# Two-layer hybrid trunk, first layer: the second half's token projections in one go, attention released behind its q part, small opening loads issued by ScalarE

## The chip, the cores and the metric

The kernel runs on one core of a Trainium2 chip. The metric is the device time of one execution in microseconds, the median of three runs. PE is TensorE, ACT is ScalarE, DVE is VectorE, POOL is GpSimd and SP is SyncE, which issues nearly all DMA transfers here.

## What is computed

Two layers over 1024 tokens of width 1024, all in float32. Each layer, shortened from the reference:

```python
xn = rmsnorm(h, attn_norm_g)
za, zq, zk, zv, zc = split(xn @ w_in)          # 512, 512, 128, 128, 256 columns
ya = chunk_gmlp(za, ...)                       # 4 heads, chunks of 128 tokens
yb = swa_sink_attention(rope(q), rope(k), v)   # 8 query heads, 2 kv heads, window 128
yc = s5_ssm(zc, ...)                           # 16 groups, then a gated output
h = h + concat[rmsnorm(ya), rmsnorm(yb), rmsnorm(yc)] @ w_out
h = h + square(relu(rmsnorm(h) @ w_ff1)) @ w_ff2          # 4096 wide
h = h + sigmoid(rmsnorm(h) @ w_ple_gate) * (p[i] @ w_ple_proj)
```

## The kernel before

The tokens are cut into two halves of 512 (h = 0 and 1), and activations stand with channels on the partitions: `X[h]` holds the input of the next product as a high and a low part (`split_scaled`, ACT for the high part at L89, DVE for the low one at L90). A product is three passes of 128x512 matmuls (`cm`, L359). Weights come through a ring: SP loads a piece of 512 KB into `st`, ACT writes its high part (L104) and DVE its low part (L105); `main_plan` fixes the order of the pieces.

The kernel is written as generators ("lanes"). `main` runs one generator and lets every other lane take steps in proportion (`tick`); flags hold a lane back (`wait`). What this emits is then put in order, engine by engine, by a scheduler, and each engine works its own list strictly in that order. SP's list matters as much as the others: a transfer that has to wait holds all transfers behind it.

The stretch that the change touches comes first. `first_x` loads x (tiles `xt`) and makes `X[0]` and `X[1]`. `project0` then does the input projection of both halves: token parts (`z_tok`, L710) give rows of tokens and have two parts, part 0 (the gMLP's v columns, k and v; weights in two pieces of 64-column strips) and part 1 (q). Channel parts (`z_chan`) give rows of channels, m = 0 and 1 for the S5 input `zu`, m = 2 and 3 for the gMLP's u, `za`. The order is: half 0 part 0, half 0 part 1, half 1 part 1 with kept weights, channel parts 0 and 1, half 1 part 0, channel parts 2 and 3. All results go to DRAM through tiles of the tag `z`, with two buffers in the pool `zs`; from the flag "zg" on, two more stand in the pool `pz`.

Beside that the lanes run: the S5 tables and `ssm(0, 0)` (it waits for the flag ("zu", 0, 0) and uses PSUM bank "x"), `gmlp(0, 0)` (bank "x" as well), and `attention(0, 0)`, which is started after "zg" and works in eight units of a block and a kv head: `pq` (L1188), `pss` (L1201), softmax, `pt` (L1238), `po` (L1259). Its outputs are written into `X[0]`, so before the first `attn_sum` it waits until the projection no longer reads `X[0]` (flag ("z", 0, 0)).

After `project0` comes `embed`: it loads p in eight tiles `ptk` (tag `z` too), transposes them (L811), and makes the products with `w_ple_proj` for both layers in 32 pieces of six matmuls, each copied by ACT to a tile `pjz` (tag `z`, L825) and stored by SP (L826). `mix_out(0, 0)` follows, the product of the three normed parts in `X[0]` with `w_out`; its first three output blocks are begun on the gMLP and attention rows alone. From there on the kernel is a row of windows, large products with the other lanes' work between them.

## Time and profile before

| what | value |
|---|---|
| median of 3 runs | 2381.09 us (2380.5 to 8480.06) |
| profiled execution, own time | 2385.95 us |
| profiled execution, span in the trace | 2384.2 us |
| PE busy over the span | 2325.3 us |
| PE idle between 0 and 300 us (from its busy time in stretches of 20 us) | 31.8 us |

A trace shows each engine's instructions with start and duration in us from the span's start, and in brackets how long the engine had been idle and what ended that. The clock PEclk is the granted TensorE clock as a share of 2.4 GHz; its lower level, 1.2 GHz, is 0.5.

### The profile page before, as it was taken

What the parts mean: (1) busy time and instruction counts of PE and PEld (TensorE: products, weight loads), DVE (VectorE), ACT (ScalarE), POOL (GpSimd) and SP (SyncE); (2) the same over time, 40 slices, a digit from 0 to 9 for tenths busy, and PEclk for the clock granted to TensorE, in tenths of its full rate; (3) what the DMA queues carried; (4) which work ended last, traced back from release to release, by engine and by line L of the source; (5) the groups of instructions that cost most, each with busy time, mean ns of one, the idle gap of its engine ahead of it and who ended that gap; (6) DMA issues with size and microseconds to landing.
All of it is one profiled execution on the core that took longest, in us unless ns stands there. A gap on an engine that the chain in (4) does not pass through costs nothing.

```text
span 2384.2 us, 29265 instructions
## 1 busy us (share of the span) xinstructions
PE 2325.3 (98%) x10941; PEld 1885.4 (79%) x10941; DVE 1552.8 (65%) x2700; ACT 1027.8 (43%) x1787; POOL 5.4 (0%) x15
## 2 busy tenths in 40 slices
PE   7998899999999999999999999999999999999998
PEld 5886687788788887777888888777888887888887
DVE  7877767675966765676585774676657674444455
ACT  7427646433334443553342543464334343322333
POOL 0000000000000000000000000000000000000000
PEclk9998999999999999999999999999999999999999
DMA  8663632253553335324443344522534334333333
GB/s 244 188 203 119 208 99 64 80 173 106 145 156 102 111 125 155 95 78 140 123 135 124 98 145 124 145 72 76 166 105 135 124 97 134 97 96 94 94 97 98
DMA packets 403558, 295.94 MB, mean 124 GB/s; under 512 B 66668, under 2 KB 376024, under 8 KB 401624
## 3 DMA queue, kind: packets, MB, share of 16 engines
q1 hardware_dynamic: 403416, 294.07, 41.1%
q8 instruction: 86, 1.41, 0.3%
q14 instruction: 56, 0.46, 0.1%
HBM read 250.48 MB, written 43.54 MB: 123 GB/s over the span
## 4 chain that ended last, share of the span: by engine, by line
PE 83%; DMA 7%; DVE 5%; ACT 3%; issue 2%; SPq 1%; ACTq 0%; DVEq 0%
PE mm_ps L359 43%; PE x_ps L359 20%; PE s_ps L359 8%; DMA st<-in_w_in 2%; DVE w L105 2%; PE s_ps L710 1%; PE po L1259 1%; PE pss L1201 1%; ACT w L104 1%; PE p_ps L359 1%; DMA st<-in_w_out 1%; PE p_ps L947 1%; DMA yu<-ye 1%; PE pt L1238 1%; SPq L98 1%
## 5 line engine op out<-in xcount | busy, mean ns | idle before, releaser
L104 ACT CAST w<-st 128x1024 fp32r<-128x1024 f32 x364 | 387.9, 1067 | 853.1 <-PE mm_ps L359 430.0
L359 PE MATMUL mm_ps<-x,w 128*128 128x512 f32 x2904 | 708.4, 396 | 7.9 <-ACT x L89 4.2
L359 PEld LDWEIGHTS mm_ps<-x,w 128*128 128x128 f32 x2904 | 544.5, 190 | 133.0 <-issue 10.1
L105 DVE TENSOR_TENSOR w<-st,w 128x1024 fp32r<-128x1024 f32 x364 | 448.5, 1234 | 202.6 <-ACT w L104 191.6
L359 PE MATMUL mm_ps<-A,w 128*128 128x512 f32 x2016 | 500.8, 392 | 2.5 <-DVE H L1333 2.5
L359 PEld LDWEIGHTS mm_ps<-A,w 128*128 128x128 f32 x2016 | 375.7, 188 | 85.4 <-DVE H L1333 4.9
L359 PE MATMUL x_ps<-A,w 128*128 128x512 f32 x1056 | 272.8, 393 | 4.1 <-DVE H L1333 4.1
L359 PE MATMUL x_ps<-x,w 128*128 128x512 f32 x1104 | 272.2, 394 | 0.0
L359 PE MATMUL s_ps<-x,w 128*128 128x512 f32 x1056 | 252.4, 391 | 4.8 <-DVE w L105 2.6
L359 PEld LDWEIGHTS x_ps<-x,w 128*128 128x128 f32 x1104 | 205.6, 188 | 45.6 <-issue 3.4
L359 PEld LDWEIGHTS s_ps<-x,w 128*128 128x128 f32 x1056 | 198.1, 188 | 49.1 <-DVE w L105 4.0
L359 PEld LDWEIGHTS x_ps<-A,w 128*128 128x128 f32 x1056 | 196.5, 188 | 51.0 <-DVE H L1333 8.3
L1333 DVE TENSOR_TENSOR H<-H,mm_ps 128x512 f32<-128x512 f32 x168 | 113.2, 683 | 84.2 <-PE mm_ps L359 83.3
L1344 DVE SCALAR_TENSOR_TENSOR r<-mm_ps,rbc 128x512 f32<-128x512 f32 x88 | 60.7, 690 | 119.2 <-PE mm_ps L359 119.2
L710 PE MATMUL s_ps<-w,x 128*128 128x512 f32 x384 | 101.3, 404 | 4.1 <-ACT x L89 2.6
L1333 DVE TENSOR_TENSOR H<-H,x_ps 128x512 f32<-128x512 f32 x88 | 60.2, 684 | 68.8 <-PE x_ps L359 68.2
L1348 DVE TENSOR_TENSOR A<-q,A 128x512 fp32r<-128x512 f32 x128 | 87.8, 686 | 6.8 <-ACT q L1347 6.6
L710 PEld LDWEIGHTS s_ps<-w,x 128*128 128x128 f32 x384 | 73.6, 194 | 20.8 <-ACT x L89 3.0
L1346 ACT ACTIVATE A<-r 128x512 fp32r<-128x512 f32 x128 | 80.2, 627 | 8.1 <-DVE r L1344 7.9
L1347 ACT ACTIVATE q<-r 128x512 f32<-128x512 f32 x128 | 78.9, 617 | 0.0
L1224 ACT ACTIVATE pr<-pr,anm,hf 128x128 f32<-128x128 f32 x128 | 61.6, 485 | 17.4 <-DVE anm L1221 17.4
L89 ACT ACTIVATE x<-H,gT 128x512 fp32r<-128x512 f32 x80 | 53.7, 711 | 13.5 <-PE s_ps L359 7.7
(386 smaller groups left out, 2112.3 us busy)
## 6 DMA issues: line engine op xcount, KB each, us to landing
st<-in_w_ff SPq DMA_DIRECT2D x256, 512.0 KB, 4.1
st<-in_w_out SPq DMA_DIRECT2D x32, 512.0 KB, 4.1
st<-in_w_ple_gate SPq DMA_DIRECT2D x32, 512.0 KB, 4.1
st<-in_w_in SPq DMA_DIRECT2D x18, 512.0 KB, 4.4
p<-par SPq DMA_DIRECT2D x8, 1024.0 KB, 8.5
pj<-pjz SPq DMA_DIRECT2D x32, 256.0 KB, 2.2
H<-hs SPq DMA_DIRECT2D x4, 2048.0 KB, 7.9
pj<-pj SPq DMA_DIRECT2D x32, 256.0 KB, 3.4
```

The lines of the kernel that those rows point to most:

```text
L89: self.S.activation(hi, x, AF.Copy, scale=g)
L98: self.Q.dma_start(sv[:, :, c0:c1], src)
L104: self.S.copy(hi, src)
L105: self.V.tensor_tensor(lo, src, hi.bitcast(F32), ALU.subtract)
L359: self.T.matmul(ps, w[:, i, k, c0:c0 + P], X[:, j, k, :], start=(start and n == 0), stop=(stop and n == last))
L710: T.matmul(pss[b], X[:, j, 2 * s + kk, c], w[:, i, kk, :], start=(s == 0 and kk == 0 and n == 0), stop=(s == 3 and kk == 1 and n == 2))
L1224: S.activation(pr[:, i], pr[:, i], AF.Exp, bias=nm[:, i:i + 1], scale=f[:, i:i + 1], accum_out=den[:, i:i + 1])
L1333: V.tensor_tensor(H[:, m], H[:, m], ps, ALU.add)
L1344: V.scalar_tensor_tensor(r, ps, 0.0, self.R[h][1], ALU.max, ALU.mult)
L1346: S.activation(A[:, 0, m], r, AF.Square)
L1347: S.activation(q, r, AF.Square)
L1348: V.tensor_tensor(A[:, 1, m], q, A.bitcast(F32)[:, 0, m], ALU.subtract)
```

## The change

Four things are edited. In `load_w` and `z_tok_plan` the four loads of 64-column strips become two, one for each 128 rows. `load_gains`, `rotary` and `ssm_tables` issue their eleven small loads from ACT. `project0` does the two token parts of half 1 one after the other, sets a new flag "zq1" after the q part, and does the four channel parts last; `run` starts the gMLP and attention lanes at "zq1", and the pool `pz` is gone. In attention the wait before the first `attn_sum` is gone; instead `attn_out` is put off until the flag is there, with two buffers for the held outputs `o` in this one place, and both pairs' factors `r` kept in one tile.

```diff
@@ load_w
         for c0, c1, src in pieces:
-            self.Q.dma_start(sv[:, :, c0:c1], src)
+            dst = sv[:, :, c0:c1]
+            if len(src.shape) == 4:
+                for k in range(a):
+                    self.Q.dma_start(dst[:, k].rearrange("p (j c) -> p j c", j=src.shape[2]), src[:, k])
+            else:
+                self.Q.dma_start(dst, src)
@@ z_tok_plan
-                pc = [(j * 64, j * 64 + 64, r[:, :, j * P + 64:(j + 1) * P]) for j in range(4)]
-                yield dict(pieces=pc + [(256, 512, r[:, :, 1024:1280])], a=2, b=512)
+                g = r[:, :, 0:512].rearrange("p k (j c) -> p k j c", j=4)[:, :, :, 64:P]
+                yield dict(pieces=[(0, 256, g), (256, 512, r[:, :, 1024:1280])], a=2, b=512)
@@ main_plan
-        chan = self.z_chan_plan(0)
-        yield next(chan)
-        yield next(chan)
         yield from self.z_tok_plan(0, 0)
-        yield from chan
+        yield from self.z_chan_plan(0)
@@ load_gains (rotary and ssm_tables alike)
-            Q.dma_start(rows[i * 16:(i + 1) * 16, :], a[nm].rearrange("l (k p) -> (l k) p", p=P))
+            S.dma_start(rows[i * 16:(i + 1) * 16, :], a[nm].rearrange("l (k p) -> (l k) p", p=P))
@@ project0
-        def chan(ms):
-            for m in ms:
-                w = F.next()
-                for h in range(2):
-                    yield from self.z_chan(0, h, m, w, "mm")
-
-        yield from chan((0, 1))
-        self.flags.add(("zu", 0, 0))
-        yield from self.z_tok(0, 1, 0, lambda s: F.next(), ss, ("p", "o", "s", "s"))
+        self.flags.add("zq1")
+        yield
+        yield from self.z_tok(0, 1, 0, lambda s: F.next(), ss, ("p", "mm", "o", "mm"))
         self.z_roots(0, 1, ss)
-        self.flags.add("zg")
-        yield
-        yield from chan((2, 3))
+        for m in range(4):
+            w = F.next()
+            for h in range(2):
+                yield from self.z_chan(0, h, m, w, "mm")
+            if m == 1:
+                self.flags.add(("zu", 0, 0))
@@ attn_steps
-                    yield from self.wait(("z", c["l"], h))
                     self.attn_sum(c, blk)
                     if blk % 2:
-                        late.append((p, blk - 1, self.attn_rstd(c)))
+                        late.append((p, blk - 1, c["o"], self.attn_rstd(c, blk % 4 // 2)))
...
-            if late and late[0][0] < p:
+            if late and late[0][0] < p and ("z", c["l"], h) in self.flags:
                 self.attn_out(c, *late.pop(0)[1:])
...
+        yield from self.wait(("z", c["l"], h))
+        for x in late:
+            self.attn_out(c, *x[1:])
+            yield
@@ attn_sum
-            c["o"] = at.tile([P, 2, 4, P], F32, name="o")
+            c["o"] = at.tile([P, 2, 4, P], F32, name="o", bufs=1 if c["l"] or c["h"] else 2)
@@ attn_rstd
-        r = c["at"].tile([P, 256], F32, tag="k", name="or")
+        if pair == 0:
+            c["r"] = c["at"].tile([P, 2, 256], F32, tag="k", name="or")
+        r = c["r"][:, pair]
@@ run
-        self.until(lambda: {"zg", "rotary"} <= self.flags)
+        self.until(lambda: {"zq1", "rotary"} <= self.flags)
         zws.close()
         self.lanes.remove(z0)
-        pzs = ExitStack()
-        self.zpools.append(self.pool(pzs, "pz", 2, side=self.side(0), reuse_waits="tile"))
...
-        self.zpools.pop()
-        pzs.close()
```

Three places of the two orders follow; lines of the changed kernel stand one to three away from those of before (L359 is L361 there, L1120 is L1118).

SP's list from its second load on, before: `pi` is the positions, `srows` and `ldr` the S5 inputs, `xt` a quarter of x.

```order
L98 DMA st<-in_w_in 128x2x64 x4
L98 DMA st<-in_w_in 128x2x256
L432 DMA rows<-in_attn_norm_g 16x128
L432 DMA rows<-in_mlp_norm_g 16x128
L432 DMA rows<-in_ple_norm_g 16x128
L432 DMA rows<-in_mix_out_g 16x128
L433 DMA rows<-in_ssm_d 4x128
L437 DMA sinks<-in_sinks 128x16
L443 DMA pi<-in_positions 8x128
L445 DMA inv<-in_inv_freq 128x32
L516 DMA srows<-in_ssm_a_re 16x128
L516 DMA srows<-in_ssm_a_im 16x128
```

And the changed kernel's, from the same place.

```order
L101 DMA st<-in_w_in 128x4x64 x2
L103 DMA st<-in_w_in 128x2x256
L477 DMA xt_196<-in_x 128x4x256
L101 DMA st<-in_w_in 128x4x64 x2
L103 DMA st<-in_w_in 128x2x256
L477 DMA xt_205<-in_x 128x4x256
```

The eleven small loads have left SP's list, and the second quarter of x moves up by thirteen issues. On ACT's list they stand before the first write of `X[0]`, five of them behind the first weight cast.

SP's list where the projection ends and `embed` begins, before (`yu` and `yt` are a store and a reload within `ssm`, `u<-za` the gMLP's load, `graw` the weights of the S5 output gate).

```order
L933 DMA graw<-in_glu_w 128x1x256 x4
L746 DMA za_138<-z 128x512
L806 DMA ptk<-in_p 128x2x256
L981 DMA u<-za_138 128x1024
L806 DMA ptk<-in_p 128x2x256
L908 DMA yu_131<-ye 128x512
L806 DMA ptk<-in_p 128x2x256
L910 DMA yt<-yu_131 128x8x64
L746 DMA za_139<-z 128x512
L806 DMA ptk<-in_p 128x2x256 x2
```

And the changed kernel's there.

```order
L748 DMA za_138<-z 128x512
L979 DMA u<-za_138 128x1024
L843 DMA u<-zu_123 128x512
L847 DMA p_2284<-par_118 128x2048
L906 DMA yu_130<-ye 128x512
L804 DMA ptk<-in_p 128x2x256
L908 DMA yt<-yu_130 128x8x64
L748 DMA za_139<-z 128x512
L804 DMA ptk<-in_p 128x2x256 x2
L103 DMA st<-in_w_out 128x8x128
L804 DMA ptk<-in_p 128x2x256 x5
```

The S5 lane now stands one half-group earlier in its own work at this place (`yu_130` is its first store, which before had gone long ago), and one `ptk` load stands ahead of the reload of `yu_130`, with seven behind it.

PE's list from the last products of `embed` to `mix_out`, before (`x_2240` is the operand of `embed`; `x_ps<-va` is the gMLP's sum of squares).

```order
L288 MATMUL x_ps<-va,onesr 128x512
L1201 MATMUL pss<-kT,qt 128x256 x8
L359 MATMUL mm_ps<-x_2240,w 128x512 x24
L1238 MATMUL pt<-identr,pr 128x128 x4
L359 MATMUL mm_ps<-x_2240,w 128x512 x12
L1259 MATMUL po<-pp,v 64x256 x2
L1259 MATMUL po<-pc,vd 64x256 x2
L1238 MATMUL pt<-identr,pr 128x128 x4
L359 MATMUL mm_ps<-x_2240,w 128x512 x12
L1259 MATMUL po<-pp,v 64x256 x2
L1259 MATMUL po<-pc,vd 64x256 x2
L359 MATMUL mm_ps<-x_2240,w 128x512 x12
```

And the changed kernel's (`x_2526` is the operand of `embed`, `x_2470` is `X[0]`).

```order
L1031 MATMUL psv<-wT,vg 64x128 x8
L361 MATMUL mm_ps<-x_2526,w 128x512 x12
L1031 MATMUL psv<-wT,vg 64x128 x8
L361 MATMUL mm_ps<-x_2526,w 128x512 x30
L290 MATMUL x_ps<-va,onesr 128x512
L361 MATMUL mm_ps<-x_2526,w 128x512 x6
L1118 MATMUL pk<-identr,kst 128x128 x20
L361 MATMUL mm_ps<-x_2470,w 128x512 x4
```

The gMLP's sum of squares now stands six matmuls ahead of the end of `embed`, where before 60 matmuls of `embed` followed it, and between `embed` and `mix_out` stand the 20 products `pk` of the next attention's keys.

## Rows read from the trace of the kernel before

**Rows 1.** Stretches: length, busy PE, PEld, DVE, ACT, POOL, PEclk, DMA share, GB/s.

```profile
0.00:50.00 50.00, 35.46 (x153) 26.83 (x153) 33.43 (x168) 40.25 (x106) 1.55 (x11) 1.00 0.78 231
102.00:183.00 81.00, 79.97 (x457) 67.16 (x456) 54.96 (x124) 25.17 (x43) 0.95 (x1) 1.00 0.72 205
183.00:211.00 28.00, 19.72 (x89) 17.20 (x88) 21.33 (x43) 20.19 (x50) 0.00 (x0) 0.70 0.45 138
211.00:289.00 78.00, 74.33 (x398) 55.03 (x397) 59.37 (x124) 60.95 (x145) 0.00 (x0) 1.00 0.45 152
289.00:294.50 5.50, 1.74 (x8) 1.12 (x6) 3.76 (x8) 1.38 (x4) 0.00 (x0) 0.84 0.85 344
339.00:365.00 26.00, 22.81 (x107) 19.04 (x106) 18.35 (x28) 15.46 (x29) 0.00 (x0) 0.92 0.26 82
```

**Rows 2.** SP's list in order of time, the opening.

```profile
1.29 2.54 SPq L98 DMA_DIRECT2D st<-in_w_in  x5
3.88 0.47 SPq L432 DMA_DIRECT2D rows<-in_attn_norm_g  x1
...
8.76 0.42 SPq L475 DMA_DIRECT2D xt<-in_x  x1
```

**Rows 3.** ACT's instructions in order of time.

```profile
9.42 1.27 ACT L89 ACTIVATE x<-mm_ps,gT 128x512 fp32r<-128x512 f32 x2 [1.43 <-DVE gT L436]
...
33.10 1.36 ACT L89 ACTIVATE x<-mm_ps,gT 128x512 fp32r<-128x512 f32 x2 [0.16 <-PE mm_ps L487]
...
185.25 0.63 ACT L212 ACTIVATE gelu_t<-u 128x512 f32<-128x512 f32 x1 [7.60 <-DMA u<-za]
```

**Rows 4.** PE's groups by line between 102 and 183 us: busy us, mean ns.

```profile
L359 PE MATMUL mm_ps<-x,w 128*128 128x512 f32 x192 | 46.1, 393 | 0.0
...
L904 PE MATMUL psY<-xp,p 128*128 128x128 f32 x32 | 5.4, 285 | 0.0
L906 PE MATMUL psY<-u,p 128*128 128x64 f32 x32 | 4.5, 262 | 0.0
```

**Rows 5.** PE's instructions in order of time.

```profile
222.70 1.19 PE L1201 MATMUL pss<-kT,qt 128*128 128x256 f32 x8
223.73 0.56 PE L1188 MATMUL pq<-identr,qst 128*128 128x128 f32 x4
...
227.04 0.65 PE L1259 MATMUL po<-pp,v 128*64 128x256 f32 x4
...
229.03 1.02 PE L288 MATMUL x_ps<-ssq,onesr 128*128 128x512 f32 x2
...
245.10 0.60 PE L1005 MATMUL pwt<-identr,wl 128*128 128x128 f32 x4
...
264.21 1.02 PE L288 MATMUL x_ps<-va,onesr 128*128 128x512 f32 x2
...
286.29 3.08 PE L359 MATMUL mm_ps<-x,w 128*128 128x512 f32 x12
289.21 1.52 PE L359 MATMUL s_ps<-x,w 128*128 128x512 f32 x6
294.52 2.07 PE L359 MATMUL mm_ps<-x,w 128*128 128x512 f32 x4 [3.78 <-ACT x L89]
```

**Rows 6.** SP's list in order of time, the first store and reload of `ssm`.

```profile
157.44 0.41 SPq L908 DMA_DIRECT2D yu<-ye  x1
...
166.06 0.37 SPq L910 DMA_DIRECT2D yt<-yu  x1
```

**Rows 7.** Instructions of the tile `pjz`: duration ns min/median/max, first and last start.

```profile
L825 ACT COPY pjz<-mm_ps x32: 563/587/650, 212.7 to 286.3; 128x512 f32<-128x512 f32 x32
...
DMA to landing us min/median/max: 2.0/2.2/6.2
```

**Rows 8.** DMA issues between 100 and 300 us: KB each, median us to landing.

```profile
ptk<-in_p SPq DMA_DIRECT2D x8, 256.0 KB, 3.4
```

**Rows 9.** DVE's instructions in order of time.

```profile
279.27 0.75 DVE L90 SCALAR_TENSOR_TENSOR x<-u,gT,x 128x512 fp32r<-128x512 f32 x1 [0.19 <-ACT x L89]
```

More of the change, by code (lines that the diff above doesn't have):

```diff
@@ L427, in load_gains @@
     def load_gains(self, t):
-        a, V, T, Q = self.a, self.V, self.T, self.Q
+        a, V, S, T = self.a, self.V, self.S, self.T
         rows = t.tile([P, P], F32, name="rows")
         for i, nm in enumerate(("attn_norm_g", "mlp_norm_g", "ple_norm_g", "mix_out_g")):
-            Q.dma_start(rows[i * 16:(i + 1) * 16, :], a[nm].rearrange("l (k p) -> (l k) p", p=P))
-        Q.dma_start(rows[64:68, :], a["ssm_d"].rearrange("l (k g) h -> (l k) (g h)", k=2))
+            S.dma_start(rows[i * 16:(i + 1) * 16, :], a[nm].rearrange("l (k p) -> (l k) p", p=P))
+        S.dma_start(rows[64:68, :], a["ssm_d"].rearrange("l (k g) h -> (l k) (g h)", k=2))
         pg = self.ps.tile([P, 512], F32, tag="t", name="pg")
@@ L436, in load_gains @@
         V.tensor_copy(self.gT, pg[:, 0:68])
-        Q.dma_start(self.sinks.rearrange("p l a -> p (l a)"), a["sinks"].rearrange("l a -> (l a)").partition_broadcast(P))
+        S.dma_start(self.sinks.rearrange("p l a -> p (l a)"), a["sinks"].rearrange("l a -> (l a)").partition_broadcast(P))
         V.tensor_scalar(self.nsk, self.sinks, -1.0, None, ALU.mult)
     def rotary(self, t):
-        a, V, T, Q = self.a, self.V, self.T, self.Q
+        a, V, S, T = self.a, self.V, self.S, self.T
         pi = t.tile([8, P], I32, name="pi")
-        Q.dma_start(pi, a["positions"][0].rearrange("(b p) -> b p", p=P))
+        S.dma_start(pi, a["positions"][0].rearrange("(b p) -> b p", p=P))
         inv = t.tile([P, 32], F32, name="inv")
-        Q.dma_start(inv, a["inv_freq"].partition_broadcast(P))
+        S.dma_start(inv, a["inv_freq"].partition_broadcast(P))
         yield
@@ L515, in ssm_tables @@
         for i, nm in enumerate(("ssm_a_re", "ssm_a_im")):
-            Q.dma_start(rows[0:N, i, :], a[nm].rearrange("l (j e) p -> (l j) (e p)", e=2))
-        Q.dma_start(ldr, a["ssm_log_dt"].rearrange("l (j e) -> (l j) e", e=2))
+            S.dma_start(rows[0:N, i, :], a[nm].rearrange("l (j e) p -> (l j) (e p)", e=2))
+        S.dma_start(ldr, a["ssm_log_dt"].rearrange("l (j e) -> (l j) e", e=2))
         yield
@@ L1273, in attn_sum, with attn_rstd, attn_out @@
         V.tensor_tensor(c["os"][:, b], sq[:, 0], sq[:, 1], ALU.add)
-    def attn_rstd(self, c):
-        r = c["at"].tile([P, 256], F32, tag="k", name="or")
+    def attn_rstd(self, c, pair):
+        if pair == 0:
+            c["r"] = c["at"].tile([P, 2, 256], F32, tag="k", name="or")
+        r = c["r"][:, pair]
         self.rstd_wide(c["os"].rearrange("p b q -> p (b q)"), 512, EPS, None, (c["at"], "rt2", 1), "t", r)
         return r
-    def attn_out(self, c, blk, r):
-        V, X, o = self.V, self.X[c["h"]], c["o"]
+    def attn_out(self, c, blk, o, r):
+        V, X = self.V, self.X[c["h"]]
         V.tensor_tensor(o, o, r.rearrange("p (b q) -> p b q", b=2).unsqueeze(2).to_broadcast([P, 2, 4, P]), ALU.mult)
```

## The prediction

> **What bounds the kernel now.** I read the page first: PE is busy nearly throughout, and what it leaves idle lies at the start. So the stretches come next [rows 1]. The first 50 us hold 14.5 us without PE work. Between 102 and 183 us, where the channel parts and the second half's part 0 run, PE lacks 1.0 us, while ACT is busy for 25 of 81 us and DVE for 55. Between 183 and 211 PE lacks 8.3 us and has a mean granted clock of 0.70, that is, some 60% of the stretch at the lower level of 1.2 GHz; spread evenly over 19.7 us of work, that costs another 5.9. Up to 289 us 3.7 are missing, up to 294.5 another 3.8, and between 339 and 365 another 3.2. Behind the opening the change can therefore win at most 20 us of waits and some 8 of low clock, about 1.2% of the run. Everything later is a row of products on a full PE, and the two orders agree again in the later windows.
>
> Which chain ends last there is told by the instructions [rows 5]: `mix_out` does 18 matmuls on the gMLP's rows (from 286.29 on), then waits 3.78 us for the last attention rows (294.52). The gMLP's rows had been written by 280.0 [rows 9]. So attention is the chain that ends last, and the gMLP has 6 us of slack before the start of `mix_out`. That slack is the question here, since the change lets attention go early and sends the S5 lane, whose PSUM bank the gMLP shares, off late.
>
> **The opening.** SP spends 2.54 us on the five pieces of a weight, and with the eleven small loads behind them the second quarter of x is issued only at 8.76 [rows 2]. With three pieces (3 x 0.51 = 1.5) and no small loads it goes at 2.8, 6 us sooner. ACT takes over eleven issues; their price there is in no row, so it lies between nothing and SP's 0.44 each ((8.76 - 3.88) / 11), 4.9 us in all. I take SP's price, the same kind of instruction. ACT is busy for 40.25 of these 50 us, and five of the eleven stand between its first weight cast and its first write of `X[0]`, which now starts at 9.42 [rows 3]. Before that, ACT idles enough to take six issues free; the other five put that write near 10.4. The squares that ACT had fitted in ahead of it come after it, and the waits for loads go. Adding up its list, the fourth pair of writes ends up at 33 to 34, where it starts at 33.1 now [rows 3]. So I book **0**: what SP gives, ACT takes. Ends: 3 us won if an issue costs ACT nothing, 5 lost if all of it lies on its path.
>
> The DMA engines are busy for 0.78 of this stretch [rows 1]. The Trainium skill (DMA: Bandwidth & Descriptors, "Issuing engines are not separate DMA queues") says that issues from several engines share the same 16 DMA engines and that only issue time is saved. By that the 3 us are a bound that needs idle DMA engines, and the booked 0 stands; were ACT's a path of its own, the 3 us would be the forecast. No run here shows it yet.
>
> **Up to the end of the projection.** The second half's part 0 and the four channel parts are the same 288 matmuls as now, in another order. Against now, one half-group of the S5 lane (`psS`, `psY`) and a `pq` leave this stretch: `psY` is 9.9 us busy for two half-groups [rows 4], so -5. Five of eight attention units come in. A `pss` occupies PE for 1.03 us from its start to the next one's [rows 5]; with `pq` (0.56), `po` (0.65 and a second one like it) and `pt`, tails overlapped, a unit is about 2.6: +13. The end, T, moves from 183 to 102 + 80 - 5 + 13 = **190**. The cover is ACT's 56 idle us and DVE's 26. If the order makes PE wait for softmax in between, T grows; between nothing and the 3.7 us that the later attention stretch shows [rows 1].
>
> **From T to the first product of `embed`.** Now this takes 28 us (183 to 211), with ACT held for 7.60 us by the gMLP's load `u<-za` and everything behind it [rows 3]. In the changed order that load is issued earlier relative to T, so this wait shrinks. Two others come in its place. The reload `yt` now stands behind the first `ptk` load and ahead of the other seven, and it waits for `yu` to land: 8.6 us the first time (157.44 to 166.06 [rows 6]), since a large load is ahead of it, as again here. With `yu` issued about T - 3.5, SP is free at T + 5. Then the pool `pz` is gone: eight `ptk` tiles go through two buffers, not four, and the second one is still held by the last `za` store, until T + 8. A round of two costs landing, 3.4 [rows 8], plus transposes and copies, about 4.3. Four rounds with the first half done: T + 8 + 4 x 4.3 = T + 25. I take **26**, and 20 to 34 as ends: rounds at 3.0 without the `yt` wait, or rounds at 4.3 after a `yu` of 8.6 from T + 3. PE has about 15 us of work for it, so some 11 us idle remain, where 8.3 are now. First product at 216.
>
> The Trainium skill (DMA: Bandwidth & Descriptors, "Anatomy of one DMA — SWDGE (gpsimd) path") gives 2.0 us plus bytes over 436 GB/s for a transfer, fitted on another issuing path; an estimate from it for 256 KB is 2.6, which would end this phase about 3 us sooner. The row says 3.4, and I go by it.
>
> **`embed` and `mix_out`.** From there to the gMLP's sum of squares stand 186 matmuls of `embed` at 0.24 [rows 4], 44.6; 24 of the S5 gate, 5.8; what is left of attention, 3.8; and small ones, 3: **57**. Two buffers for `pjz` give one piece in (0.59 copy + 0.4 issue + 2.2 landing [rows 6, 7]) / 2 = 1.6 us, 51 for 32 pieces, inside the 57. Bank "x" costs more: S5's sum of squares to the gMLP's first product in that bank takes 16.1 us (229.03 to 245.10 [rows 5]), all of it the S5 lane's root on ACT and DVE; the changed order leaves 42 matmuls between them, 10 us. DVE is less crowded then, so I put the stall at 4, and 2 for the gMLP's steps behind the next attention's `k` and gain loads, which DVE's list now has ahead of them: +6. The sum of squares comes at 216 + 57 + 6 = 279. From it to the gMLP's rows in `X[0]` it takes 280.0 - 264.2 = 15.8 [rows 5, 9]. `mix_out` starts at **294.8**; the 20 key products fill part of that wait at no cost.
>
> Now `mix_out` resumes at 294.5 with 18 matmuls done, 4.3 us, as if it had started at 290.2: so 4.6 us lost. Given back: the key products and their waits are done ahead of the 339 to 365 stretch, of whose 3.2 us I take 3. Sum: 0 + 4.6 - 3 = **+1.6**. The attention chain is won, the S5 and gMLP chain takes its place.
>
> The profiled execution took 2385.95 of its own time (span 2384.2) and would take 2387.5; it lies 4.9 above the median, so against the median, 2381.09 + 1.6 = **2382.7**.
>
> **The rivals.** *Faster*: the chain from S5's sum of squares to the gMLP's rows took 51 us (229.0 to 280.0) because attention's softmax shared ACT and DVE; freed of it, bank "x" causes no stall (-6), the last leg takes 10, not 15.8, and the `ptk` phase ends at T + 20. `mix_out` starts 6 + 5.8 + 6 = 18 us sooner: 2382.7 - 18 = 2365; with the opening's 3, 2362. For it: ACT's busy share between 211 and 289 is 61 of 78, much of it softmax. Against it: the next attention's key work and weight splits stand in that last leg. *Slower*, one mechanism: two `z` buffers where four stood. It decides once a `pjz` store takes over 2.6 us to land: 32 x (0.59 + 0.4 + x) / 2 exceeds 57. The rows reach 6.2 [rows 7]. At the 3.4 of `ptk`, 70 us replace 57 + 6, and `ptk` ends at T + 34: + 7 + 8 gives 2398. *The change's opening does what it says and costs*: ACT's issues lie on its path, 5 us: 2388. That attention is not let go is excluded by the order, which has five units ahead of T.
>
> **How the numbers follow.** The forecast, 2373 to 2390 with the costly opening in it, has 0.47; faster, 2355 to 2372, 0.28; slower, 2391 to 2405, 0.20; anything else 0.05. Reaching into both, the range is 2360 to 2399. None of these reaches 2% (48 us), about what a measurement of this kernel can tell from no change: the whole pool of waits is 28 us behind the opening, and the slower case costs 15. So same 0.96, faster 0.02, slower 0.02.
>
> **What would show it.** In the changed profile: the second quarter of x issued near 2.8, the first write of `X[0]` by ACT at 10 to 11; the projection's last matmul near 190 with attention units among the channel parts; a clock below 1 just after it, with `ptk` issues spread over 20 to 26 us; the gMLP's sum of squares as the last product but six of `embed`, then an idle PE before `mix_out`, released by ACT or DVE writing the gMLP's rows; and no such wait for attention rows. Wrong would be: `mix_out` at 277 or before (the chain shortened), PE waiting for `pjz` copies again and again (two buffers), or PE waiting for softmax before 190.

## The result and the profile after

The changed kernel takes 2413.55 us (median of 4 runs, 2410.81 to 2416.49) against 2381.48 for the kernel before: 1.0128 times as long, with a 95% interval of 1.0115 to 1.0141. The ratio leaves out one execution of the kernel before that took 8480 us and is not the quotient of these two medians, which is 1.0135. Forecast were 2382.7 and a range that ended at 2399; the time lies above every case that the prediction named. The difference is clear of the scatter, but under the 2% (48 us) below which the prediction counted a time as the same, as it did this one with 0.96. The profiled execution has a span of 2413.8 where before has 2384.2, 29.6 more.

The stretches of the changed kernel, columns as in [rows 1], cut at its own ends: opening, from the q part to the last channel product, to the first product of `embed`, to the gMLP's sum of squares, to the start of `mix_out`.

```profile
0.00:50.00 50.00, 30.96 (x117) 23.53 (x118) 31.61 (x151) 37.56 (x101) 1.55 (x11) 0.90 0.78 230
109.00:208.20 99.20, 93.56 (x497) 75.56 (x495) 71.35 (x170) 48.54 (x123) 0.95 (x1) 0.95 0.54 160
208.20:238.40 30.20, 19.97 (x138) 15.51 (x138) 24.83 (x54) 15.81 (x32) 0.00 (x0) 0.77 0.45 135
238.40:309.40 71.00, 63.77 (x289) 47.05 (x289) 43.48 (x86) 40.48 (x84) 0.00 (x0) 0.95 0.53 169
309.40:323.60 14.20, 4.98 (x21) 4.09 (x19) 11.95 (x20) 8.46 (x21) 0.00 (x0) 0.61 0.43 131
```

PE lacks 19.0 us in the first 50, where it lacked 14.5, and 5.6 in a stretch that was nearly full before. Every stage loses some us, and none carries the loss alone. PE's list shows where they end:

```profile
13.38 2.08 PE L712 MATMUL s_ps<-w,x 128*128 128x512 f32 x4
...
107.54 1.53 PE L712 MATMUL p_ps<-w,x 128*128 128x512 f32 x6
...
136.28 8.36 PE L361 MATMUL mm_ps<-x,w 128*128 128x512 f32 x24 [3.82 <-DVE hss L703]
...
147.51 6.23 PE L361 MATMUL mm_ps<-x,w 128*128 128x512 f32 x19 [0.61 <-DVE hss L703]
...
176.25 0.62 PE L859 MATMUL psS<-u,p 128*64 128x64 f32 x13
...
207.64 0.62 PE L361 MATMUL mm_ps<-x,w 128*128 128x512 f32 x2
...
238.40 3.03 PE L361 MATMUL mm_ps<-x,w 128*128 128x512 f32 x12
...
269.73 1.02 PE L290 MATMUL x_ps<-ssq,onesr 128*128 128x512 f32 x2
...
280.98 4.61 PE L361 MATMUL mm_ps<-x,w 128*128 128x512 f32 x12 [2.84 <-ACT pjz L823]
...
301.01 1.85 PE L361 MATMUL mm_ps<-x,w 128*128 128x512 f32 x6 [3.83 <-ACT pjz L823]
...
307.14 1.02 PE L290 MATMUL x_ps<-va,onesr 128*128 128x512 f32 x2
...
323.66 2.07 PE L361 MATMUL mm_ps<-x,w 128*128 128x512 f32 x4 [0.24 <-ACT x L89]
```

The first row is the first token product, the second is where the q part ends. At 136.28 the first channel product waits for the sum over heads (`hss`) that frees an `mm` bank, and the 24 products behind it take 8.36 us. The granted clock says why (same columns as above): a mean of 0.67 there and 0.73 in the next such piece, where the 22 us behind them have 1.00.

```profile
136.20:144.70 8.50, 8.43 (x27) 6.76 (x28) 3.47 (x6) 2.84 (x6) 0.00 (x0) 0.67 1.07 330
147.50:153.80 6.30, 6.29 (x22) 5.05 (x23) 6.00 (x25) 0.14 (x1) 0.00 (x0) 0.73 0.32 83
154.00:176.00 22.00, 22.00 (x119) 18.81 (x117) 15.57 (x30) 11.74 (x33) 0.00 (x0) 1.00 0.42 108
```

Three more rows of PE in the kernel before stand beside these, the first token product, the end of the q part and the S5 lane's first product, `psS`:

```profile
10.22 2.08 PE L710 MATMUL s_ps<-w,x 128*128 128x512 f32 x4
...
101.90 1.52 PE L710 MATMUL p_ps<-w,x 128*128 128x512 f32 x6
...
137.21 1.15 PE L861 MATMUL psS<-u,p 128*64 128x64 f32 x32
```

`psS` stands at 176.25 in the changed kernel, 39 us later. The lane's sum of squares (`ssq`) follows at 269.73 (229.03 in [rows 5]), the gMLP's at 307.14 (264.21), and `mix_out` starts at 323.66, not at 294.52. ACT's row that releases it is the gMLP's (`x<-u`), where before it was attention's (`x<-o`). The changed kernel, then before:

```profile
322.88 0.72 ACT L89 ACTIVATE x<-u,gT 128x512 fp32r<-128x512 f32 x1 [0.76 <-DVE u L1047]
```

```profile
293.96 0.91 ACT L89 ACTIVATE x<-o,gT 128x256 fp32r<-128x256 f32 x2 [2.27 <-DVE o L1282]
```

So attention is indeed no longer the chain that ends last, and the S5 and gMLP chain is, as I said. From the first `psS` to the start of `mix_out` it takes 147.4 us. Before, it took 142.8 to the gMLP's rows (137.2 to 280.0, [rows 9]). Its length hardly changed; it starts 39 us later.

### The profile page after: what moved, and what is told of

The parts are those of the page before. It is cut to its first block, busy times and chain, and to the rows that moved or that the text cites. A ratio compares the mean times of both kernels' runs of the same rounds, so it can differ in the third digit from the quotient of the medians.

```text
span 2413.8 us, 29219 instructions
## 1 busy us (share of the span) xinstructions
PE 2336.6 (97%) x10941; PEld 1891.6 (78%) x10941; DVE 1553.0 (64%) x2700; ACT 1027.1 (43%) x1787; POOL 5.4 (0%) x15
## 4 chain that ended last, share of the span: by engine, by line
PE 84%; DMA 7%; DVE 4%; ACT 3%; issue 1%; SPq 0%; ACTq 0%; DVEq 0%
PE mm_ps L361 44%; PE x_ps L361 20%; PE s_ps L361 8%; DMA st<-in_w_in 3%; DVE w L110 1%; ACT w L109 1%; PE s_ps L712 1%; PE po L1260 1%; PE p_ps L361 1%; PE pss L1202 1%; DMA st<-in_w_out 1%; DMA ptk<-in_p 1%; PE o_ps L712 1%; DMA pj<-pjz 1%; PE p_ps L945 1%
## 5 line engine op out<-in xcount | busy, mean ns | idle before, releaser
L361 PE MATMUL mm_ps<-x,w 128*128 128x512 f32 x2904 | 713.3, 398 | 12.4 <-ACT pjz L823 7.1
L361 PEld LDWEIGHTS mm_ps<-x,w 128*128 128x128 f32 x2904 | 547.6, 191 | 137.9 <-ACT pjz L823 10.1
L361 PE MATMUL mm_ps<-A,w 128*128 128x512 f32 x2016 | 501.0, 392 | 1.3 <-DVE H L1336 1.3
L361 PEld LDWEIGHTS mm_ps<-A,w 128*128 128x128 f32 x2016 | 376.1, 188 | 84.5 <-issue 4.1
L361 PE MATMUL x_ps<-A,w 128*128 128x512 f32 x1056 | 273.3, 394 | 5.0 <-DVE H L1336 5.0
L361 PE MATMUL x_ps<-x,w 128*128 128x512 f32 x1104 | 273.0, 395 | 0.0
L361 PE MATMUL s_ps<-x,w 128*128 128x512 f32 x1056 | 252.0, 391 | 3.6 <-DVE w L110 1.4
L361 PEld LDWEIGHTS x_ps<-x,w 128*128 128x128 f32 x1104 | 205.9, 188 | 46.5 <-issue 4.6
L361 PEld LDWEIGHTS x_ps<-A,w 128*128 128x128 f32 x1056 | 196.3, 188 | 53.2 <-DVE H L1336 10.3
L361 PEld LDWEIGHTS s_ps<-x,w 128*128 128x128 f32 x1056 | 198.1, 188 | 47.8 <-DVE w L110 2.6
L712 PE MATMUL s_ps<-w,x 128*128 128x512 f32 x336 | 87.8, 400 | 1.9 <-ACT x L89 1.9
L1349 ACT ACTIVATE A<-r 128x512 fp32r<-128x512 f32 x128 | 80.1, 626 | 14.7 <-DVE r L1347 14.5
L712 PEld LDWEIGHTS s_ps<-w,x 128*128 128x128 f32 x336 | 63.7, 192 | 15.5 <-ACT x L89 2.4
```

The costliest lines, as they stand in the source:

```text
L361: self.T.matmul(ps, w[:, i, k, c0:c0 + P], X[:, j, k, :], start=(start and n == 0), stop=(stop and n == last))
L712: T.matmul(pss[b], X[:, j, 2 * s + kk, c], w[:, i, kk, :], start=(s == 0 and kk == 0 and n == 0), stop=(s == 3 and kk == 1 and n == 2))
L1349: S.activation(A[:, 0, m], r, AF.Square)
```

## The experiments

Eighteen kernels, each timed against the kernel before. "Opening" is ScalarE's issues and merged strips, "order" the token parts in one go with the banks `p`, `mm`, `o`, `mm` for part 0, "early" attention let go behind the q part. The kernel before itself ran from 2376 to 2387 us in these sessions, so steps of 2 or 3 us between kernels are not read. Each edit also changes what the scheduler makes of the rest: `banks_before` differs from the kernel before by four bank names, yet by their traces only about two thirds of PE's instructions in the first 600 us stand in the same order in both. So two kernels differ by an edit and by the new order that comes of it.

| run | what it has | us | ratio, 95% interval |
|---|---|---|---|
| proj_only | order, early, no pool; old opening | 2406.1 | 1.0098, 1.0072 to 1.0124 |
| open_only | opening alone | 2389.0 | 1.0030, 1.0018 to 1.0043 |
| acts_only | ScalarE's issues alone | 2389.6 | 1.0027, 1.0016 to 1.0039 |
| strips_only | merged strips alone | 2372.3 | 0.9958, 0.9940 to 0.9976 |
| banks | proj_only, banks p, mm, o, x | 2403.6 | 1.0092, 1.0067 to 1.0117 |
| tok_only | order alone | 2399.6 | 1.0073, 1.0057 to 1.0088 |
| att_only | early, no pool, new banks; old order | 2399.9 | 1.0078, 1.0060 to 1.0097 |
| nopz | pool `pz` taken away alone | 2390.3 | 1.0035, 1.0020 to 1.0050 |
| pool_only | small loads on GpSimd | 2386.6 | 1.0022, 1.0011 to 1.0034 |
| strips_pool | the same with merged strips | 2392.6 | 1.0044, 1.0029 to 1.0059 |
| tok_mm | tok_only, gMLP on `mm` | 2396.7 | 1.0062, 1.0047 to 1.0078 |
| pz1 | proj_only, pool back | 2404.8 | 1.0095, 1.0079 to 1.0111 |
| att_pz1 | att_only, pool back | 2375.7 | 0.9973, 0.9960 to 0.9986 |
| tok_oldbanks | tok_only, old banks | 2379.3 | 0.9989, 0.9977 to 1.0001 |
| acts_late | 8 of 11 loads on ScalarE | 2384.0 | 1.0013, 1.0004 to 1.0022 |
| banks_before | new banks alone | 2387.8 | 1.0026, 1.0013 to 1.0039 |
| strips_att | strips_only and att_pz1 | 2386.4 | 1.0024, 1.0014 to 1.0033 |
| strips_tok | strips_only and tok_oldbanks | 2389.2 | 1.0032, 1.0020 to 1.0044 |

### The change cut in two, and the opening again

`proj_only` is the changed kernel with the lines of the opening as before; `open_only` is the kernel before with them changed, `acts_only` with the first of these two edits and its like for all eleven loads, `strips_only` with the second:

```diff
-            Q.dma_start(rows[i * 16:(i + 1) * 16, :], ...)
+            S.dma_start(rows[i * 16:(i + 1) * 16, :], ...)
```

```diff
-                pc = [(j * 64, j * 64 + 64, r[:, :, j * P + 64:(j + 1) * P]) for j in range(4)]
-                yield dict(pieces=pc + [(256, 512, r[:, :, 1024:1280])], a=2, b=512)
+                g = r[:, :, 0:512].rearrange("p k (j c) -> p k j c", j=4)[:, :, :, 64:P]
+                yield dict(pieces=[(0, 256, g), (256, 512, r[:, :, 1024:1280])], a=2, b=512)
```

> The changed kernel with its opening put back: the five pieces of a strip and SP's issues of the eleven small loads as before. The trace of the changed kernel has its q part end some 7 us later than before (108.9 against 101.9) and loses 22.6 more behind it. Theory (the two parts of the change cost independently): q part back at 102, and a time some 7 us under the changed kernel's, near 2406. Rival (the delay of the opening is made up or caused by the later order; the opening is free): within 2 us of 2413. Rival (the opening is what upsets the later order): near the kernel before, under 2395.

> The kernel before with the opening's edits alone (ScalarE's issues and the merged strips). Theory: its SP list, too, has the loads of the S5 tables ahead of the last quarters of x, and ScalarE holds five issues ahead of its first write of X[0]; the q part ends 6 to 7 us later and the run takes 2387 to 2389. Rival (the opening is free, as I had booked it): 2380 to 2383. Rival (the opening pays where the later order is the old one): under 2379.

> The kernel before with the eleven small loads on ScalarE, strips in five pieces. If ScalarE's issues are what the opening costs (five of them ahead of the first write of X[0], some 2 us, and the loads of the S5 tables let in early): first write of X[0] near 12, and 3 to 7 us slower, 2384 to 2388. If the merged strips are the cost: within 1 us of before, 2380 to 2382.5, or up to 3 faster, since the second x quarter goes out at about 4.

> The kernel before with the strips merged from five pieces to three, small loads on SP as before. If the merged pieces are what the opening costs (the first strip of the changed kernel took 5.6 us from its last issue to landing): the first weight cast starts after 7.5 and the run is 3 to 7 us slower. If ScalarE's issues are the cost: within 1 us of before or 1 to 2 us faster, 2379 to 2382.5, since SP saves some 1 us per strip.

The opening costs 7.2 by itself (before took 2381.8 there) and 7.5 in the changed kernel (2413.6 less 2406.1), so its price does not hang on the rest of the change. Its two halves go opposite ways, merged strips win 9.5 (2 at most were expected) and ScalarE's issues cost 7.8, and they do not add: on top of merged strips the issues cost 17. In `acts_only` the first write of `X[0]` comes at 10.49, not near 12 as I expected; PE's first products wait for a small load instead (PE, then ACT's list):

```profile
12.19 0.28 PE L522 MATMUL pt<-identr,srows 16*128 16x16 f32 x1 [1.92 <-DMA srows<-in_ssm_a_re]
...
12.73 2.07 PE L710 MATMUL s_ps<-w,x 128*128 128x512 f32 x4
```

```profile
7.93 1.04 ACT L104 CAST w<-st 128x1024 fp32r<-128x1024 f32 x1 [4.86 <-DMA st<-in_w_in]
7.96 0.33 ACTq L516 DMA_DIRECT2D srows<-in_ssm_a_re  x1
```

The S5 tables' loads (`srows`) stand in ACT's list behind a weight cast that waits 4.86 us for its strip. They land late, and their transposes stand ahead of PE's first token product: 12.73 where before has 10.22. The price of an issue (0.29 to 0.49) is small beside what it is queued behind. Two kernels ask for that: all eleven loads on GpSimd, which is idle there (`pool_only`), and `acts_only` with the loads of `srows` (two) and `ldr` back on SP (`acts_late`).

```diff
-            Q.dma_start(rows[0:N, i, :], ...)
+            self.G.dma_start(rows[0:N, i, :], ...)
```

```diff
-            S.dma_start(rows[0:N, i, :], ...)
+            Q.dma_start(rows[0:N, i, :], ...)
```

> The kernel before with the eleven small loads issued by GpSimd, which is idle there (1.55 us busy), strips in five pieces. With ScalarE as the issuer the same edit costs 7.8 us. Theory (ScalarE's row is the cost: the loads of the S5 tables stand there behind a weight cast that waits for its strip, and hold up PE's first products): no such wait, first token product at 10.5 or before, 2373 to 2382. Rival (the big loads that SP now issues ahead of the small ones are the cost, whoever issues those): first token product at 12 or later, 2386 to 2391.

> Eight of the eleven small loads on ScalarE, the three of the S5 tables on SP (acts_only, with all eleven, took 2389.6). Theory (a load issued behind a weight cast in ScalarE's row is the cost): PE does not wait for srows, first token product near 10.5, 2379 to 2384. Rival (what costs is that SP's big loads come ahead, squares and casts being put ahead of the writes of X): 2386 to 2391.

`strips_pool` is `pool_only` with the strips merged.

> The kernel before with the merged strips and the small loads on GpSimd. Merged strips alone took 2372.3. If ScalarE's row was the only cost of moving the loads: 2364 to 2372. If taking them off SP costs by itself: 2376 to 2385.

`pool_only` went the rival's way, by another wait (ACT's list, then PE):

```profile
10.68 0.42 ACT L496 ACTIVATE sq<-xt 128x256 f32<-128x256 f32 x1
...
13.19 1.04 ACT L104 CAST w<-st 128x1024 fp32r<-128x1024 f32 x1 [2.01 <-DMA st<-in_w_in]
14.14 1.26 ACT L89 ACTIVATE x<-mm_ps,gT 128x512 fp32r<-128x512 f32 x2
```

```profile
14.88 2.08 PE L710 MATMUL s_ps<-w,x 128*128 128x512 f32 x4 [6.22 <-ACT x L89]
```

With SP free of small loads the second quarter of x goes out at 3.88, so the list puts its four squares and the second weight cast ahead of the first write of `X[0]`. On the chip that cast waits until 13.19. In `acts_late` the loads of `srows` land earlier (PE still waits 1.34 and 1.42 us for them, but its second transpose of `srows` is at 10.17, where `acts_only` has 12.51): first token product at 10.39, last channel product at 182.9 (192.3 in `acts_only`), 5.6 us back. Where the remaining 3.6 are is not shown: the last channel product (183.2 before) and the start of `mix_out` (294.8, 294.5 before) are level with the kernel before. So the theory of the list stands for ScalarE, and its rival, by another wait, for GpSimd: with all small loads off SP, big loads and what hangs on them stand ahead of PE's first product. In `strips_pool` that wait is 8.69 us, the first token product comes at 18.52, and the strips' gain is lost.

### The order, the banks and the pool

`tok_only` is the kernel before with the order of the changed one, attention let go behind part 0 as before and the pool kept. Part 0's banks are changed in `banks` (on `proj_only`, first line put in) and `tok_oldbanks` (on `tok_only`, second line); `banks_before` puts the removed line's banks into the kernel before, in its own order. `nopz` takes the pool from the kernel before.

```diff
-        yield from self.z_tok(0, 1, 0, lambda s: F.next(), ss, ("p", "mm", "o", "mm"))
+        yield from self.z_tok(0, 1, 0, lambda s: F.next(), ss, ("p", "mm", "o", "x"))
+        yield from self.z_tok(0, 1, 0, lambda s: F.next(), ss, ("p", "o", "s", "s"))
```

```diff
-        self.zpools.append(self.pool(pzs, "pz", 2, side=self.side(0), reuse_waits="tile"))
```

> The changed kernel with the old opening, and the fourth PSUM bank of the second half's part 0 taken from x in place of mm. In the run with the old opening alone PE waits 3.66 and 0.63 us for the sums of squares that free the two mm banks, 1.1 for key work behind it, and runs 40 of the 192 channel products near half clock (51.5 us busy where before has 46.1). Theory (that handover is the largest piece of the loss): the waits of 3.66 and 0.63 go, the last channel product ends near 192 instead of 201, and the time falls by 7 to 11, to 2395 to 2399. Rival (the end is set later, by the two z buffers and the late gMLP): last channel product earlier, first product of mix_out unmoved near 315, 2403 to 2407.

> The kernel before with the token parts of the second half in one go, its banks and the channel parts behind them; attention still let go behind the last token product, pool pz kept. If the new order is what costs (mm banks handed over late, S5 inputs stored late): a wait of some 3.7 us for hss, first product of mix_out later than 300, 2390 to 2400. If early attention and the missing pool are the cost: within 4 us of before, 2378 to 2386.

> The kernel before without the pool pz: two z buffers from the channel parts to the end of embed, nothing else changed. The changed kernel's stores of pjz go through SP in one row and its copies wait for them (waits of 2.84 and 3.83 us on PE). If two buffers are a cost of their own: the eight ptk loads spread over 20 us or more, PE waits for pjz copies add up to 8 us or more, and the time is 8 to 15 longer, 2390 to 2397. If the 1.6 us per piece that I worked out are hidden: within 3 us, 2379 to 2385.

> The new order of the parts alone (tok_only, 2399.6), with the old kernel's four banks p, o, s, s for part 0, which nobody else holds since attention starts behind it. If the handover of the mm banks is what the new order costs (a wait of 3.5 us and channel products near half clock behind it): wait gone, last channel product at 184 to 186, 2386 to 2392. If the late S5 lane is: 2396 to 2402 with mix_out still waiting for rows near 300.

> The kernel before with nothing but the banks of part 0 changed from p, o, s, s to the changed kernel's p, mm, o, mm. If the handover costs wherever channel products follow part 0: a wait for hss of 3 us or more at the third channel part and 4 to 9 us longer, 2386 to 2391. If it costs only with the weights and gMLP steps that the new order puts beside it: within 2 us, 2380 to 2385.

`tok_only` costs 17 (before took 2382.7 there) without early attention and with the pool; with the old banks the same order costs nothing (2379.3). This pair holds the largest term: the order with the old banks is free, with its own banks it is not. The time is below the 2386 to 2392 that I expected from the banks alone. PE in `tok_only`, then in `tok_oldbanks`:

```profile
130.20 7.33 PE L356 MATMUL mm_ps<-x,w 128*128 128x512 f32 x24 [3.52 <-DVE hss L698]
...
163.53 0.92 PE L854 MATMUL psS<-u,p 128*64 128x64 f32 x24
...
256.84 1.02 PE L285 MATMUL x_ps<-ssq,onesr 128*128 128x512 f32 x2
...
302.01 2.07 PE L356 MATMUL mm_ps<-x,w 128*128 128x512 f32 x4 [13.28 <-ACT x L89]
```

```profile
153.80 0.69 PE L854 MATMUL psS<-u,p 128*64 128x64 f32 x16
...
233.57 1.02 PE L285 MATMUL x_ps<-ssq,onesr 128*128 128x512 f32 x2
...
283.00 1.20 PE L356 MATMUL mm_ps<-x,w 128*128 128x512 f32 x4 [2.29 <-ACT x L89]
```

The wait for `hss` and the half clock behind it put the last channel product at 190.4 and not at 182.9; `psS` comes 10 later and `mix_out` 19. So the later `psS` is about half of the 19; the other half is a longer way from `psS` to `mix_out` (138.5 and 129.2), and its cause is not shown. In `banks` the `hss` wait behind part 0 is gone, but with early attention others come in its place (1.44 us for keys, 1.78 for ACT's `qt`, 0.96 for a `z` buffer, 0.61 for a weight), 20 channel products take 7.61 us, and the last one ends at 200.0 (201.0 in `proj_only`): 2.5 won where 7 to 11 were expected. `banks_before` shows no `hss` wait behind part 0: in the old order the banks do not stall PE there. It still took 7 longer, a time that I had expected only together with that wait, and its trace does not tell why.

`nopz` costs 8, the lower end of what I expected: PE waits for copies of `pjz` add up to 7.1 us between 252 and 292 (3.7 before), the longest 4.34, and `embed` begins at 214.6 (211.1 before).

### Early attention, and the gMLP's bank

`att_only` is the kernel before with the changed kernel's `attn_steps`, `attn_sum`, `attn_rstd` and `attn_out`, `zq1` set ahead of its own order of parts, the new banks and no pool. `att_pz1` and `pz1` give the pool back to it and to `proj_only`, in the room of the second held output:

```diff
-            c["o"] = at.tile([P, 2, 4, P], F32, name="o", bufs=1 if c["l"] or c["h"] else 2)
+            c["o"] = at.tile([P, 2, 4, P], F32, name="o")
...
                 if gk == 1:
+                    if late:
+                        yield from self.wait(("z", c["l"], h))
+                        self.attn_out(c, *late.pop(0)[1:])
```

`tok_mm` is `tok_only` with another bank for the gMLP:

```diff
-        self.lane(self.gmlp(0, 0, 0, "x", [("attn", 0, 0)]), RATE0)
+        self.lane(self.gmlp(0, 0, 0, "mm", [("attn", 0, 0)]), RATE0)
```

> The kernel before with its own order (channel parts 0 and 1, part 0, channel parts 2 and 3), but attention let go behind the q part with held outputs, the banks of the changed kernel for part 0 and no pool pz. If early attention or the missing pool is the cost: 2390 or more. If the order is: attention's wait of 3.78 us at mix_out goes and S5 starts as early as before, 2372 to 2380.

> The old order of the parts with attention let go behind the q part, one held output and the pool pz (att_only with its second output given back; 2399.9 there). Theory (early attention by itself is neutral, the missing buffers cost some 8 us and embed's stores take the place of the attention that is gone from under it): embed's 32 pieces in under 62 us where att_only takes 69.6, and 2388 to 2393. Rival (early attention costs by itself, since embed has less to hide its stores behind): pieces still 2.2 us apart, 2395 to 2402. Rival (it pays, as the change meant): under 2381.

> The changed kernel with the old opening (2406.1), the pool pz put back in the room of the second held output; attention's second pair then waits for the last channel part. Theory (two buffers cost some 8 us, as in the kernel before without pz): 2396 to 2400, ptk loads spread over under 15 us. Rival (the buffers were hidden behind the late S5 lane here): 2403 to 2408. Rival (early attention pays once the buffers are there): under 2393.

> The new order of the token parts alone (tok_only, 2399.6) with the gMLP's PSUM tiles taken from mm in place of x, the bank that it shares with the S5 lane. In tok_only mix_out waits 13.28 us for the gMLP's rows. Theory (the S5 lane, started later by the new order, holds bank x while the gMLP needs it): the gMLP's sum of squares comes 10 us or more sooner, mix_out waits under 6 us, 2386 to 2393. Rival (the gMLP is late for its own inputs or for ACT and DVE): sum of squares within 4 us of 283.6, 2396 to 2402.

In the old order early attention pays, if the pool stays: `att_pz1` is 4.8 under the kernel before, `att_only`, without the pool and with a second held output, 17 over it. The two changes between these kernels were not tried apart. The difference stands in `embed`: its 32 copies of `pjz` run from 241.75 to 311.39 without the pool, 2.25 apiece, and from 231.53 to 286.64 with it, 1.78. In neither does `mix_out` wait for rows at its start. In the changed order the pool does not help (`pz1`): `psS` at 162.9, last channel product 10 us sooner than in `proj_only`, `mix_out` 10 sooner, yet only 1.2 in the median. At the first products of the second feed-forward matrix 8.9 of the 10 are still there (389.5 against 398.3), and at the end of the profiled executions 4.2 (2402.0 against 2406.2); what takes them back behind this stretch was not followed.

`tok_mm` gives the gMLP a bank of its own. Its sum of squares comes at 239 instead of 284, and the time falls by 3 only: now `embed` itself ends last (its copies run from 222.3 to 300.5). So the shared bank is what ties the gMLP to the S5 lane. Untying it uncovers another bound, or makes one: `embed` works in `mm` too, its copies start 6.7 later than in `tok_only` and take 3.9 longer.

### The parts that paid, put together

`strips_att` is `att_pz1` with merged strips, `strips_tok` is `tok_oldbanks` with them.

> The kernel before with the two parts that paid: merged strips (2372.3 alone) and attention let go behind the q part in the old order, with one held output and the pool pz (2375.7 alone); small loads on SP. If the two gains are of different stretches they add: 9 and 5 off, 2365 to 2369. If both come from the same start of mix_out: 2370 to 2374. If the lists move against each other, as with strips_pool: above 2376.

> The changed kernel's merged strips and order of the token parts, with the old banks, attention let go behind part 0, pz kept and the small loads on SP. The order with these banks took 2379.3. If the strips' gain adds: 2368 to 2373. If it is lost in the new order: 2376 to 2382.

Neither adds up. `strips_att` is 14 over `strips_only`: PE waits twice for `hss` (1.24 and 2.01), and the last channel product falls to 221.6 (213.0 in `att_pz1`). `strips_tok`, above both ranges that I gave, has everything up to `embed` as early as `tok_oldbanks` (last channel product 182.4, first `embed` product 211.8), but the S5 lane's `ssq` 13 later, and PE waits:

```profile
153.22 0.33 PE L859 MATMUL psS<-u,p 128*64 128x64 f32 x2
...
246.81 1.02 PE L290 MATMUL x_ps<-ssq,onesr 128*128 128x512 f32 x2
...
296.95 2.07 PE L361 MATMUL mm_ps<-x,w 128*128 128x512 f32 x4 [15.15 <-ACT x L89]
```

The fastest of all is `strips_only`, 9.5 us under the kernel before and 41 under the changed one.

## Why the prediction was wrong

It held that the attention chain is won and the S5 and gMLP chain takes its place. The size did not, and for a time outside the three cases I had left 0.05: `mix_out` starts at 323.7, and I had 294.8. The 28.9 go to four steps:

| step | predicted | measured | off by |
|---|---|---|---|
| the opening, end of the q part | 102 | 107.5 | 5.5 |
| from there to T, the last channel product | 88 | 100.7 | 12.7 |
| T to the first product of `embed` | 26 | 30.2 | 4.2 |
| `embed` to the gMLP's sum of squares, then to its rows | 63 + 15.8 | 68.7 + 16.5 | 6.4 |

**Opening, booked at 0.** SP did nearly what I said: the second quarter of x went out at 3.55, where I had 2.8 and before has 8.76. But the first write of `X[0]` came at 12.44, not at 10.4, and the fourth pair ended at 37.8, not at 33 to 34 (ACT, as in [rows 3]):

```profile
12.44 1.26 ACT L89 ACTIVATE x<-mm_ps,gT 128x512 fp32r<-128x512 f32 x2
...
37.15 0.68 ACT L89 ACTIVATE x<-mm_ps,gT 128x512 fp32r<-128x512 f32 x1
```

The first token product stands at 13.38 and not at 10.22, PE lacks 4.5 us more in the first 50 than before, and its mean granted clock there is 0.90, where [rows 1] have 1.00. I priced ScalarE's issues by their number; the runs showed that their place in the list counts. In both kernels that moved the loads, the first strip, issued at 1.29 as before, lands later (its cast starts at 7.93 in `acts_only` and 7.54 in `pool_only`, at 6.94 before), and the second, issued sooner, lands sooner (its cast, which waits for it in all three, starts at 14.73 and 13.19, at 15.72 before). The Trainium skill (DMA: Bandwidth & Descriptors, "Issuing engines are not separate DMA queues") says that transfers issued by several engines run interleaved on the same 16 DMA engines and that only the time to issue is saved; both casts agree with it. The strips, which I counted as two issues saved on SP and no more, win 9.5 alone.

**T = 190, the step that failed most.** "The same 288 matmuls as now, in another order", and attention's units on top: I counted work, and looked for waits only at softmax. I did not ask who frees the banks. The counted work nearly came out: apart from the channel products, PE is busy 9.6 us longer on this way than before (41.8 and 32.2), where I had 8. What I had at nothing is the wait for a bank and the low clock behind it. Part 0 now uses `mm`, which the channel products need next, and the release stands behind a weight cast (ACT, then DVE, changed kernel):

```profile
131.96 1.95 ACT L109 CAST w<-st 128x1024 fp32r<-128x1024 f32 x1 [3.05 <-DMA st<-in_w_in]
133.81 0.68 ACT L699 ACTIVATE z<-p_ps,rtm 128x512 f32<-128x512 f32 x1
134.39 0.68 ACT L699 ACTIVATE z<-mm_ps,rtm 128x512 f32<-128x512 f32 x1
135.21 0.35 ACT L702 ACTIVATE mm_ps<-mm_ps,rtm 128x128 f32<-128x128 f32 x1
```

```profile
133.94 1.89 DVE L110 TENSOR_TENSOR w<-st,w 128x1024 fp32r<-128x1024 f32 x1 [0.52 <-ACT w L109]
135.94 0.28 DVE L703 TENSOR_REDUCE hss<-mm_ps 128x2 f32<-128x128 f32 x1
```

Waits on that way are 3.82 + 0.61, and 1.20 for key work between them; the 192 channel products are busy for 51.9 us where [rows 4] have 46.1: 11.4 together. `tok_only` against `tok_oldbanks` shows that the banks, and not the order by itself, are what the new order costs. That the `hss` wait and the clock behind it are all of that price is not shown: `banks`, without this wait, won 2.5, and `banks_before` lost 7 without it.

**T to `embed`.** Forecast 26 with ends 20 to 34, measured 30.2. The `yt` wait and the rounds of `ptk` loads came as described (SP's list):

```profile
203.48 0.36 SPq L906 DMA_DIRECT2D yu<-ye  x1
203.88 0.43 SPq L804 DMA_DIRECT2D ptk<-in_p  x1
...
209.86 0.37 SPq L908 DMA_DIRECT2D yt<-yu  x1
...
215.48 10.10 SPq L804 DMA_DIRECT2D ptk<-in_p  x5
```

`nopz` puts the price of two buffers at 8 in the kernel before, so the rival that had them cost 15 more was right in kind there. In the changed order giving them back (`pz1`) won 1.2, less than is read here.

**`embed` and `mix_out`.** I booked 6 us of waits here, for bank "x" and for the gMLP's steps behind the next attention's, and none for the copies of `pjz`. The trace has it the other way round: between 238.4 and 309.4 PE waits nowhere for the S5 lane or the gMLP, and 7.1 us for copies of `pjz`. That was my sign of the two buffers, but the longest of these waits, 3.83, is another: the copy stands on ACT's list behind a weight cast that waits for its load.

```profile
299.42 1.05 ACT L109 CAST w<-st 128x1024 fp32r<-128x1024 f32 x1 [3.42 <-DMA st<-in_w_out]
300.38 0.58 ACT L823 COPY pjz<-mm_ps 128x512 f32<-128x512 f32 x1
```

The same lateness can be counted along the S5 lane. I had placed it by counting matmuls between its products in PE's list. Read as a chain with a length of its own, it starts behind the store of the first two channel parts, which the new order moves. These are the runs in which the gMLP's rows release `mix_out`, in order of that start:

| run | first `psS` | `ssq` | `mix_out` | from `psS` on | us |
|---|---|---|---|---|---|
| strips_tok | 153.2 | 246.8 | 297.0 | 143.7 | 2389.2 |
| tok_oldbanks | 153.8 | 233.6 | 283.0 | 129.2 | 2379.3 |
| pz1 | 162.9 | 254.7 | 305.3 | 142.4 | 2404.8 |
| tok_only | 163.5 | 256.8 | 302.0 | 138.5 | 2399.6 |
| banks | 169.8 | 258.9 | 310.2 | 140.4 | 2403.6 |
| proj_only | 172.5 | 264.4 | 315.3 | 142.8 | 2406.1 |
| changed kernel | 176.3 | 269.7 | 323.7 | 147.4 | 2413.6 |

In six of seven the chain takes 138 to 147 us, whether attention comes early, late, with two buffers or four. To the gMLP's sum of squares it is 115 to 131 us from the first `psS` in every kernel of this document but `tok_mm`, old order or new, with `psS` anywhere from 133 to 176. From the 142.8 of before and a start at 176.3 the profile alone would have given 319. What pushed the start by 39: 16.6 the order (153.8), 9.7 its banks (163.5), 9.0 early attention without the pool (172.5; with the pool and one held output it is 162.9), 3.8 the opening. That the length of the lane sets the end is read from this regularity and not shown: everything behind `psS` in PE's list moves with it too. That the chain is 129 in `tok_oldbanks`, and 144 from nearly the same start once strips are merged, stays open; so does why the strips' 1.0 us at the q part's end (100.9) becomes 10 at `mix_out` (284.1).

One reading of the prediction was a little off: [rows 9] show the first half of the gMLP's rows; the second is written by 281.5, so the 6 us of slack were nearer to 5.

**Given back.** 3 were booked; the changed kernel's `mix_out` is 33.5 behind the 290.2 that I took as its effective start before, and its end 29.6: 3.9.

## What to carry to other kernels

Before work is moved in a list, follow each chain that hangs on it from its first store to its last consumer, take its length from the trace, and add it to the new start. As a first estimate this came within 5 us in the changed kernel and within 14 in the worst case of the table; slack read at the chain's end (10 us here, from 280.0 to 290.2) is about what the start may move. Where the moved work uses a shared bank or buffer, look at what stands ahead of its release on the other engines' lists; here the old list of banks made the same order free. A small DMA issued from a computing engine is as late as whatever that engine waits for ahead of it.

## What the runs showed of the hardware that I had not expected

With ScalarE issuing beside it, SP's five pieces of the first two strips took 4.25 and 6.13 us to issue (`acts_only`), with no more bytes than before, where the first took 2.54 ([rows 2]) and with GpSimd issuing 2.54 and 2.56. Each issue is still 0.37 to 0.51 long; the rest is SP standing still, for the most part until an earlier transfer of x (3.1 us) or of a strip (2.0) has landed, though no data ties them. Whether the chip or the program's own semaphores hold it was not tried.

```profile
1.29 4.25 SPq L98 DMA_DIRECT2D st<-in_w_in  x5
...
6.09 6.13 SPq L98 DMA_DIRECT2D st<-in_w_in  x5
```

GpSimd's issues are in the trace as busy instructions of 0.48 to 0.62 us each, where SP's take 0.33 to 0.51.
